# A macaron layer on one core: later sums for the first pair of quarters in the first FFN, and plain products for the second pair in its fourth chunk

## The chip, the core and the metric

The kernel runs on one core of one Trainium2 chip. The time is the device time of that core in microseconds (us), from the first to the last instruction with what lies around it. The kernel before takes 2368.13 us, the median of three runs (2365.34 to 2368.92).

The engines named below: TensorE (PE in the rows; PEld is its weight load), VectorE (DVE), ScalarE (ACT), GpSimd (POOL), and SyncE (SP), whose queue issues all DMAs of this kernel.

## The reference, cut to what matters

One encoder layer is applied to 1024 prompt frames and 32 sample frames, side by side as 1056 columns of 1024 channels. Its first step, where the change lies, is a half-step SwiGLU FFN:

```python
def _swiglu_half_step(x, g_pre, g_post, w_in, w_out):
    h = _rmsnorm(x, g_pre)
    gate, up = jnp.split(h @ w_in, 2, axis=-1)
    return x + 0.5 * _rmsnorm((jax.nn.silu(gate) * up) @ w_out, g_post)
```

D_FF is 2816, so `w_in` gives 22 chunks of 128 gate rows and 128 up rows. All inputs are float32. After this FFN come a mixing part (convolution and RG-LRU branches), a second FFN of the same form and a last norm.

## The kernel before

**Precision.** Each float32 operand is split into a high part and a low part (`split`, L84: ScalarE copies the high part, then VectorE subtracts it from the operand). A product is three matmuls (`mm3`, L204 to L206): high by high, high by low, low by high.

**Columns.** The 1056 columns are four quarters of 264 (q = 0 to 3); quarters 0 and 1 are the first pair, 2 and 3 the second.

**Two ways to form a chunk.** *Plain products* (`gemm`): for each quarter the gate row and the up row take 8 k-steps each, so one pair of quarters costs 2 x 2 x 8 x 3 = 96 matmuls. They read the chunk's two weight blocks, each split over 1024 columns into `wh_i`, `wl_i`. *Seven products* (`swiglu`): a pair of quarters is treated as a 2 x 2 block product with seven instead of eight block products, 7 x 4 x 3 = 84 matmuls. They need seven weight operands (`w_ops`, `w1` to `w7`) and seven column operands `xh1`..`xh7`, `xl1`..`xl7` of the pair. Parts 1, 2 and 3 are split from the normed quarters; 4 to 7 come from sums of them (`x_sums`: four sums into `t` or `f`, each followed by a split). `swiglu` runs the products in the order 1, 5, 6, 2, 7, 3, 4 on four PSUM banks; a copy on ScalarE and an add on VectorE stand between them.

**The first FFN's start.** The first three chunks (`NP[0]` = 3) take plain products for all four quarters, quarter by quarter, while the operands of the other 19 are made. Quarters 0 and 1 go in with only the gain applied; their norm factor is put in afterwards on the products (`held`, `rows`), and their column parts are built later (`build`, with `f_a0`, `f_a1`). Quarters 2 and 3 are normed first: squares on ScalarE (`sq_a`), their sum on VectorE (`ss_a`), a matmul with ones (`pst`, L230), `r_a` on VectorE, a power on GpSimd (`q_a`, L234), a transpose on TensorE (`pst`, L240), then eight multiplications (`f_a`, L270) and the splits. Quarter 3's first half is split into `xhp`, `xlp` (needed by the plain products) and its second into `xh3`, `xl3`.

**What sets the order.** The program's order is a priority: a scheduler keeps it on each engine except where `tc.high_priority`, `tc.issue_after` or free buffers move an instruction. So what the loop over q emits first on VectorE is first there. `x_sums` of the first pair (with the builds before it) is emitted after quarter 1's products, and `first(3, h)`, quarter 3's norm, is emitted at the start of quarter 2's turn:

```python
            late = first(q + 1, h) if q + 1 < NQ else None
            ...
            c = {1: 0, 3: 1}.get(q) if n == 1 else {2: 0, 3: 1}.get(q)
            if c is not None:
                while builds:
                    builds.pop(0)()
                x_sums(x[c], f[2 * c], f[2 * c + 1], f"{n}_{c}")
```

**Buffers.** Raw weight blocks have 3 buffers (`w_i`, `w_g`, `w_u`), split weights a ring of 12 (`NRING`), PSUM banks 6. A DMA on the SP queue waits there until its buffer is free, and everything behind it waits too. `WAHEAD` and `WLATE` say how far ahead of its place a chunk's `w_ops` is put.

Of the kernel before, what the change touches and what calls it, by code (L numbers as in the profile page):

```python
# [10 lines left out]
AF = mybir.ActivationFunctionType  # L11
OP = mybir.AluOpType
# [8 lines left out]
N = T // NQ  # L21
# [15 lines left out]
AHEAD, WAHEAD, WLATE, HAHEAD, OAHEAD, EAHEAD = 350, 120, 100, 100, 150, 200  # L37
# [17 lines left out]
def macaron_kernel(ctx: ExitStack, tc: tile.TileContext, a: dict, o: dict):  # L55
    nc = tc.nc
# [26 lines left out]
    def TMP(name):  # L83
        return tp.tile([P, N], F32, tag="t", name=name)  # L84
# [4 lines left out]
    def tt(out, x, y, op):  # L89
        return nc.vector.tensor_tensor(out, x, y, op=op)  # L90
# [125 lines left out]
    def gemm(blk, h, q, name):  # L216
        b = BANK(name)[:, :N]
        while q not in h:
            later.pop(0)[1]()
        for k in range(KC):  # L220
            hi, lo = h[q][k // HC]
            mm(b, blk, k, hi[:, k % HC, :], lo[:, k % HC, :], k == 0, k == KC - 1)
        return b
# [132 lines left out]
    def x_sums(r, fe, fo, name):  # L356
        t = QUAD(F32, f"t_{name}")

        def op(k, v):
            r[k] = (QUAD(F32R, f"xh{k}_{name}"), QUAD(F32R, f"xl{k}_{name}"))  # L360
            split(*r[k], v)

        tt(t, fo[0], fe[0], OP.subtract)
        op("5", t)
        tt(t, fo[1], t, OP.subtract)
        op("6", t)
        tt(fo[0], fo[1], fo[0], OP.subtract)
        op("7", fo[0])
        tt(t, fe[1], t, OP.subtract)
        op("4", t)  # L370

    def w_ops(g, u, name, ahead):
        r = {}
        with tc.high_priority(offset=ahead):
            wg, wu = raw_block(g, f"g{name}"), raw_block(u, f"u{name}")
            H = D // 2
            a11, a12, a21, a22 = wg[:, :H], wg[:, H:], wu[:, :H], wu[:, H:]

            def op(k, v):
                r[k] = ring.tile([P, 2, H], F32R, tag="r", name=f"w{k}_{name}")  # L380
                split(r[k][:, 0, :], r[k][:, 1, :], v)

            def mid(n):
                return mp.tile([P, H], F32, tag="m", name=f"{n}_{name}", padded_shape=[P, 2 * N])

            op("1", a11)
            op("2", a12)
            op("4", a22)
            s = mid("s")
            tt(s, a21, a22, OP.add)  # L390
            op("5", s)
            tt(s, s, a11, OP.subtract)
            op("6", s)
            s3 = mid("s3")
            tt(s3, a11, a21, OP.subtract)
            tt(s, a12, s, OP.subtract)
            op("7", s3)
            op("3", s)
        return r
# [64 lines left out]
    def ffn(x, f, h, first, mid, w_in, w_out, early, between, finish, tail, n):  # L464
        hd = dp.tile([NF, P, T], F32, name=f"hd{n}")

        def hidden(i, w, cs):
            cols = [(x[c], MID(f"prod{n}_{i}_{c}")) for c in cs]
            last = swiglu(w, cols, f"{n}_{i}_{cs[0]}")
            for c, (_, prod) in zip(cs, cols):  # L470
                nc.sync.dma_start(hd[i, :, 2 * N * c:2 * N * (c + 1)], prod)
            return last

        blks = []

        def in_block(i, j):
            blks.append(block(w_in[2 * i + j], f"i{n}_{i}_{j}", AHEAD if n == 2 else 0, 0 if n == 2 else 2000 if i or j else 4000))

        if n == 1:
            late = first(0, h, lambda: in_block(0, 0))  # L480
        else:
            late = first(0, h)
        q0 = list(newest_part) if n == 1 else []
        np = NP[n - 1]
        for i in range(np):
            for j in range(2):
                if 2 * i + j == len(blks):
                    with behind_parts(q0):
                        in_block(i, j)
        held, rows = {}, {}  # L490
        for q in range(NQ):
            if late:
                held[q] = []
                late(held, rows)
            late = first(q + 1, h) if q + 1 < NQ else None
            if q not in h:
                drain()
            for i in range(np):
                pg = gemm(blks[2 * i], h, q, f"pg{n}_{i}_{q}")
                pu = gemm(blks[2 * i + 1], h, q, f"pu{n}_{i}_{q}")  # L500

                def gate(i=i, q=q, pg=pg, pu=pu, rows=rows):
                    t = TMP(f"si{n}_{i}_{q}")
                    if q in held:
                        u = TMP(f"su{n}_{i}_{q}")
                        tt(t, rows[q], pg, OP.mult)
                        tt(u, rows[q], pu, OP.mult)
                        pg, pu = t, u
                    nc.scalar.activation(t, pg, AF.Silu)
                    tt(t, t, pu, OP.mult)  # L510
                    nc.sync.dma_start(hd[i, :, q * N:(q + 1) * N], t)

                if q in held and q not in rows:
                    held[q].append(gate)
                else:
                    gate()
            c = {1: 0, 3: 1}.get(q) if n == 1 else {2: 0, 3: 1}.get(q)
            if c is not None:
                while builds:
                    builds.pop(0)()  # L520
                x_sums(x[c], f[2 * c], f[2 * c + 1], f"{n}_{c}")
        for i in range(np, NF):
            with behind_parts(q0 if i == np else []):
                w = w_ops(w_in[2 * i], w_in[2 * i + 1], f"{n}_{i}", WAHEAD if i < np + 2 else WLATE)
            for cs in ((0,), (1,)) if i == np else ((0, 1),):
                end = hidden(i, w, cs)
            if i == 4:
                with tc.issue_after(end):
                    mid()

        sq = {}
        for c in range(2):
            hid = []
            for g in range(NF // 2):
                with tc.high_priority(offset=HAHEAD):
                    w = PAIR(F32, f"hf{n}_{c}_{g}")
                    nc.sync.dma_start(w, hd[2 * g:2 * g + 2, :, 2 * N * c:2 * N * (c + 1)].rearrange("k p n -> p k n"))
                    hi, lo = PAIR(F32R, f"hh{n}_{c}_{g}"), PAIR(F32R, f"hl{n}_{c}_{g}")
                    split(hi, lo, w)
                hid.append((hi, lo))  # L540
            y = {q: [QUAD(F32, f"y{n}_{q}_{h}") for h in range(2)] for q in (2 * c, 2 * c + 1)}
            for t in (t for q in y for t in y[q]):
                nc.gpsimd.memset(t[:, 0, 0:1], 0.0)
            if c == 1:
                for q in y0:
                    after(q * STAG, lambda q=q, y0=y0: early(q, y0[q], sq[q]))
            y0 = y

            def out(tiles, blks, which, c=c, hid=hid, y=y):

                b = {t: BANK(f"po{n}_{t[0]}_{t[1]}")[:, :N] for t in tiles}
                for k in range(NF):
                    hi, lo = hid[k // 2]
                    for m, q in tiles:
                        i = m * NF + k
                        if i // KC not in blks:
                            blks[i // KC] = block(w_out[i // KC], f"o{n}_{which}_{i // KC}", OAHEAD)
                        s = slice((q % 2) * N, (q % 2 + 1) * N)
                        mm(b[m, q], blks[i // KC], i % KC, hi[:, k % 2, s], lo[:, k % 2, s], k == 0, k == NF - 1)
                for m, q in tiles:  # L560
                    evacuate(y[q], m, b[m, q], half[:, n - 1, m:m + 1], sq, q, f"{n}_{q}_{m}")

            qs = (2 * c, 2 * c + 1)
            late = tail if c == 1 else 0
            both = {}
            out([(m, q) for m in range(OG) for q in qs], both, c)
            for m in range(OG, KC - late):
                for q in qs:
                    out([(m, q)], both, c)
                if c == 1 and m == HC - 1:  # L570
                    between()
            for q in qs:
                own = {}
                for m in range(KC - late, KC):
                    out([(m, q)], own, f"{c}_{q}")
                if c == 1 and q == 2:
                    finish(q, y[q], sq[q])
        return lambda: finish(3, y[3], sq[3])
# [62 lines left out]
    rows = {}  # L641
# [39 lines left out]
    w_in = a["w_in"]  # L681
# [81 lines left out]
    for i in range(KC):  # L763
# [3 lines left out]
        if first:  # L767
            u = ROW(F32, f"u{i}")
# [27 lines left out]
        else:  # L796
            u = ROW(F32, f"u{i}")
# [156 lines left out]
    for c in range(2):  # L954
        blks = {}
# [4 lines left out]
        for q in (2 * c, 2 * c + 1):  # L960
            blks = {}
# [75 lines left out]
```

## Time and profile before

| | us |
|---|---|
| median of three runs | 2368.13 |
| the profiled execution | 2366.67 |
| its span, first to last instruction | 2364.9 |
| TensorE busy in the span | 2323.3 (98%) |
| VectorE, ScalarE, GpSimd busy | 1466.2, 988.5, 41.6 |

The profiled execution lies 1.46 us under the median and 1.8 us over its own span. Its mean granted TensorE clock is 0.993 of full speed. A matmul's duration in the rows (0.28 us) overlaps its neighbours', so its cost is the distance from start to start. In the rows of a timeline the columns are start, duration, engine, line, operation, output and inputs, shapes, count, and in brackets the idle time before it with what ended it.

### The profile page before, as it was taken

How to read it: one execution, taken by the hardware profiler on the slowest of the kernel's cores; microseconds unless marked ns; L12 is line 12 of the kernel's file. 1: busy time of each engine (PE TensorE's matmuls, PEld its weight loads, DVE VectorE, ACT ScalarE, POOL GpSimd, SP SyncE). 2: the span in 40 equal slices, each digit the busy share in tenths (PEclk: the TensorE clock that was granted, in tenths of full speed). 3: DMA queues.
4: the chain of work that ended last, by engine and by line, in shares of the span. 5: the costliest groups of instructions: out<-in, count | busy, mean ns of one | idle time of the engine just before them, and what ended most of it. 6: DMA issues, size and time to landing. Idle time of an engine off the chain costs nothing.

```text
span 2364.9 us, 44868 instructions
## 1 busy us (share of the span) xinstructions
PE 2323.3 (98%) x19136; PEld 2318.4 (98%) x19136; DVE 1466.2 (62%) x2289; ACT 988.5 (42%) x1709; POOL 41.6 (2%) x63
## 2 busy tenths in 40 slices
PE   8799999999999999999999999999999999999996
PEld 8799999999999999999999999999999999999996
DVE  6764444542656887887778966458744444552646
ACT  4443333442444554355543434244433333442432
POOL 0000000000000000000000000001000000000000
PEclk9899999999999999999999999999999999999998
DMA  4122222353656222222122554444222222353554
GB/s 173 50 83 82 76 79 82 106 195 116 202 184 192 74 82 78 70 90 83 65 72 84 184 192 157 146 135 154 77 74 78 82 79 76 120 188 108 169 173 130
DMA packets 126088, 274.12 MB, mean 116 GB/s; under 512 B 16704, under 2 KB 58432, under 8 KB 125888
## 3 DMA queue, kind: packets, MB, share of 16 engines
q1 hardware_dynamic: 125888, 271.26, 34.3%
q8 instruction: 149, 2.44, 0.4%
q14 instruction: 51, 0.42, 0.1%
HBM read 212.55 MB, written 58.67 MB: 115 GB/s over the span
## 4 chain that ended last, share of the span: by engine, by line
PE 95%; DVE 2%; issue 1%; DMA 1%; ACT 0%; POOL 0%; SPq 0%; POOLq 0%; DVEq 0%
PE p L204 11%; PE p L206 11%; PE p L205 11%; PE po L205 7%; PE po L204 7%; PE po L206 7%; PE pm L204 3%; PE pm L206 3%; PE pm L205 3%; PE pcv L204 1%; PE pco L204 1%; PE pcg L204 1%; PE pro L204 1%; PE prx L204 1%; PE prg L204 1%; PE pcg L206 1%
## 5 line engine op out<-in xcount | busy, mean ns | idle before, releaser
L206 PE MATMUL p<-xh,w 128*128 128x264 f32 x2184 | 617.4, 283 | 0.0
L205 PE MATMUL p<-xl,w 128*128 128x264 f32 x2184 | 617.3, 283 | 0.0
L204 PE MATMUL p<-xh,w 128*128 128x264 f32 x2184 | 614.5, 284 | 0.0
L205 PEld LDWEIGHTS p<-xl,w 128*128 128x128 f32 x2184 | 410.8, 188 | 0.0
L206 PEld LDWEIGHTS p<-xh,w 128*128 128x128 f32 x2184 | 410.2, 188 | 0.0
L204 PEld LDWEIGHTS p<-xh,w 128*128 128x128 f32 x2184 | 407.8, 188 | 0.4 <-ACT p L93 0.2
L205 PE MATMUL po<-hl,wh_o 128*128 128x264 f32 x1408 | 398.0, 285 | 0.2
L206 PE MATMUL po<-hh,wl_o 128*128 128x264 f32 x1408 | 396.6, 284 | 0.0
L204 PE MATMUL po<-hh,wh_o 128*128 128x264 f32 x1408 | 391.7, 286 | 0.0
L205 PEld LDWEIGHTS po<-hl,wh_o 128*128 128x128 f32 x1408 | 264.8, 188 | 0.9 <-DVE hl L90 0.9
L206 PEld LDWEIGHTS po<-hh,wl_o 128*128 128x128 f32 x1408 | 264.4, 188 | 0.0
L204 PEld LDWEIGHTS po<-hh,wh_o 128*128 128x128 f32 x1408 | 260.8, 188 | 0.3 <-ACT hh L93 0.2
L90 DVE TENSOR_TENSOR wl_o<-w_o,wh_o 128x1024 fp32r<-128x1024 f32 x109 | 133.0, 1223 | 117.2 <-ACT wh_o L93 116.9
L90 DVE TENSOR_TENSOR p<-p,s 128x264 f32<-128x264 f32 x78 | 34.2, 441 | 273.0 <-ACT p L93 273.0
L709 DVE SCALAR_TENSOR_TENSOR pq<-u,vec,pq 128x542 f32<-128x542 f32 (+14 forms) x232 | 170.7, 767 | 0.0
L93 ACT ACTIVATE wh_o<-w_o 128x1024 fp32r<-128x1024 f32 x109 | 115.3, 1063 | 121.5 <-PE po L205 111.6
L90 DVE TENSOR_TENSOR w<-s,w 128x512 fp32r<-128x512 f32 x156 | 104.4, 690 | 76.3 <-ACT w L93 76.1
L93 ACT ACTIVATE p<-p 128x264 f32<-128x264 f32 x156 | 58.3, 374 | 198.1 <-PE p L206 197.0
L93 ACT ACTIVATE w<-s 128x512 fp32r<-128x512 f32 x156 | 94.0, 626 | 81.7 <-DVE s L90 79.1
L709 DVE SCALAR_TENSOR_TENSOR rs<-rs,wsum 128x542 f32<-128x542 f32 (+6 forms) x112 | 86.0, 768 | 0.0
L90 DVE TENSOR_TENSOR s<-s,s 128x264 f32<-128x264 f32 x56 | 24.0, 429 | 99.1 <-ACT s L315 98.9
L90 DVE TENSOR_TENSOR hl<-hf,hh 128x1056 fp32r<-128x1056 f32 x44 | 55.2, 1254 | 44.5 <-ACT hh L93 44.4
(465 smaller groups left out, 5680.8 us busy)
## 6 DMA issues: line engine op xcount, KB each, us to landing
w_o<-in_w_ffn_out SPq DMA_DIRECT2D x109, 512.0 KB, 3.7
hf<-hd SPq DMA_DIRECT2D x44, 528.0 KB, 4.9
hd<-prod SPq DMA_DIRECT2D x78, 264.0 KB, 2.0
w_g<-in_w_ffn_in SPq DMA_DIRECT2D x39, 512.0 KB, 3.5
w_u<-in_w_ffn_in SPq DMA_DIRECT2D x39, 512.0 KB, 3.4
w_wo<-in_w_out SPq DMA_DIRECT2D x18, 512.0 KB, 3.6
sgd<-sg SPq DMA_DIRECT2D x32, 264.0 KB, 2.5
gs<-sgd SPq DMA_DIRECT2D x16, 528.0 KB, 6.7
```

The costliest lines, as they stand in the source:

```text
L90: return nc.vector.tensor_tensor(out, x, y, op=op)
L93: return nc.scalar.activation(out, x, AF.Copy)
L204: nc.tensor.matmul(out, wh, xh, start=first, stop=False, skip_group_check=True)
L205: nc.tensor.matmul(out, wh, xl, start=False, stop=False, skip_group_check=True)
L206: newest_mm[:] = [nc.tensor.matmul(out, wl, xh, start=False, stop=last, skip_group_check=True).ins]
L709: nc.vector.scalar_tensor_tensor(acc[c][:, d:], src[c][:, :HW - d], wt[c](d), acc[c][:, d:], op0=OP.mult, op1=OP.add)
```

## The change

In the first FFN the first pair's builds and sums are emitted after quarter 2's products instead of after quarter 1's. The second FFN already had that place. The body that forms a plain chunk becomes a function `plain(i, q)`, the same lines as before. After the loop over the quarters, two more blocks of weights (the fourth chunk's, `i` = 3) are loaded and split, and that chunk takes plain products for quarters 2 and 3; its seven products are then run for the first pair alone. The chunk that runs its two pairs one after the other instead of interleaved is now the fifth.

```diff
             for i in range(np):
...
-            c = {1: 0, 3: 1}.get(q) if n == 1 else {2: 0, 3: 1}.get(q)
+                plain(i, q)
+            c = {2: 0, 3: 1}.get(q)
             if c is not None:
                 while builds:
                     builds.pop(0)()
                 x_sums(x[c], f[2 * c], f[2 * c + 1], f"{n}_{c}")
+        both = np
+        if n == 1:
+
+            both = np + 1
+            for j in range(2):
+                in_block(np, j)
+            for q in (2, 3):
+                plain(np, q)
         for i in range(np, NF):
             with behind_parts(q0 if i == np else []):
-                w = w_ops(w_in[2 * i], w_in[2 * i + 1], f"{n}_{i}", WAHEAD if i < np + 2 else WLATE)
-            for cs in ((0,), (1,)) if i == np else ((0, 1),):
+                w = w_ops(w_in[2 * i], w_in[2 * i + 1], f"{n}_{i}", WAHEAD if i < both + 2 else WLATE)
+            for cs in ((0,),) if i < both else ((0,), (1,)) if i == both else ((0, 1),):
                 end = hidden(i, w, cs)
```

**VectorE, from the end of quarter 1 to the sum of squares of quarter 3.** In the names `f_a1`, `sq_a3` the digit is the quarter; `xl5_1_0` is part 5 of the first pair in the first FFN. Before:

```order
L270 SCALAR_TENSOR_TENSOR f_a1_1_660<-x0_1_1_90,vec_87,rb_a1_506 128x264 x4
L90 TENSOR_TENSOR xl3_1_1_666<-f_a1_1_660,xh3_1_1_665 128x4x264
L90 TENSOR_TENSOR t_1_0_669<-f_a1_0_655,f_a0_0_637 128x4x264
L90 TENSOR_TENSOR sq_a3_0_690<-sq_a3_0_690,sq_a3_2_692 128x528
L90 TENSOR_TENSOR f_a1_0_655<-f_a1_1_660,f_a1_0_655 128x4x264
L90 TENSOR_TENSOR xl5_1_0_672<-t_1_0_669,xh5_1_0_671 128x4x264
L90 TENSOR_TENSOR sq_a3_0_690<-sq_a3_0_690,sq_a3_4_695 128x528
L90 TENSOR_TENSOR t_1_0_669<-f_a1_1_660,t_1_0_669 128x4x264
```

The changed kernel has there, on VectorE:

```order
L90 TENSOR_TENSOR su1_2_1_631<-rb_a1_506,pu1_2_1_605 128x264
L90 TENSOR_TENSOR sq_a3_0_637<-sq_a3_0_637,sq_a3_2_639 128x528
L90 TENSOR_TENSOR si1_2_1_630<-si1_2_1_630,su1_2_1_631 128x264
L90 TENSOR_TENSOR sq_a3_0_637<-sq_a3_0_637,sq_a3_4_642 128x528
L90 TENSOR_TENSOR sq_a3_0_637<-sq_a3_0_637,sq_a3_6_645 128x528
L90 TENSOR_TENSOR ss_a3_648<-sq_a3_0_637 128x264
L232 TENSOR_SCALAR r_a3_692<-pst_a3_688 88x3
L90 TENSOR_TENSOR si1_0_2_708<-si1_0_2_708,pu1_0_2_675 128x264
L270 SCALAR_TENSOR_TENSOR f_a3_0_722<-x0_3_0_177,vec_87,pst_a3_688 128x264 x4
L90 TENSOR_TENSOR xlp_1_3_728<-f_a3_0_722,xhp_1_3_727 128x4x264
```

Quarter 3's squares and its `f_a3` now stand directly behind quarter 1's last gate; the builds of quarters 0 and 1 and all sums of the first pair stand behind them.

With them quarter 3's ones-matmuls (`pst`, L230) and transposes (L240) on TensorE move from behind quarter 2's last product into its first products, some 100 matmuls forward.

**VectorE, in the fourth chunk's seven products for the first pair, in the changed kernel.** `w7_1_3` and `w3_1_3` are weight operands of the fourth chunk (chunk index 3), `w1_1_4` of the fifth; `p6`, `p7` are PSUM banks; `xl6_1_1` to `xl4_1_1` are parts of the second pair.

```order
L90 TENSOR_TENSOR w7_1_3_1222<-s3_1_3_1219,w7_1_3_1222 128x512
L90 TENSOR_TENSOR xl6_1_1_1064<-t_1_1_1056,xh6_1_1_1063 128x4x264
L90 TENSOR_TENSOR si1_3_2_1139<-si1_3_2_1139,pu1_3_2_1114 128x264
L90 TENSOR_TENSOR p6_1_3_0_0_1242<-p6_1_3_0_0_1242,s5_1_3_0_0_1257 128x264
L90 TENSOR_TENSOR xl7_1_1_1069<-f_a3_0_722,xh7_1_1_1068 128x4x264
L90 TENSOR_TENSOR t_1_1_1056<-f_a2_1_539,t_1_1_1056 128x4x264
L90 TENSOR_TENSOR prod1_3_0_1228<-p7_1_3_0_0_1271,s5_1_3_0_0_1257 128x264
L90 TENSOR_TENSOR w3_1_3_1225<-s_1_3_1210,w3_1_3_1225 128x512
L90 TENSOR_TENSOR w1_1_4_1333<-w_g1_4_1329,w1_1_4_1333 128x512
```

Splits of the second pair stand between the steps that this chunk's products wait for; before, the second pair's last split stands in front of the chunk's first step.

**SP, the queue of DMAs.** The two new weight loads are put among the loads of quarters 2 and 3:

```order
 L174 DMA w_i_2_1_167<-in_w_ffn_in 128x1024
+L174 DMA w_i_3_0_1077<-in_w_ffn_in 128x1024
 L113 DMA x_2_0_173<-in_x 128x4x264
+L174 DMA w_i_3_1_1083<-in_w_ffn_in 128x1024
 L113 DMA x_2_1_174<-in_x 128x4x264
```

Three of the four loads of x (quarter 2's second half and quarter 3) now stand behind two weight loads, the first half of quarter 2 behind one. The order of TensorE from the sixth chunk's first product on is the same row by row.

## Rows read from the trace of the kernel before

**Rows 1.** The page, part 1: busy time, share of the span, instructions.

```profile
PE 2323.3 (98%) x19136; PEld 2318.4 (98%) x19136; DVE 1466.2 (62%) x2289; ACT 988.5 (42%) x1709; POOL 41.6 (2%) x63
```

**Rows 2.** Waits of TensorE up to 300 us: waiter, releaser, us in total, times, longest.

```profile
PE pst_a L230 <- DVE ss_a L90: 8.0, 1, 8.0
PE pg L204 <- ACT xhp L93: 2.9, 1, 2.9
PE pst_a L240 <- POOL q_a L234: 1.2, 1, 1.2
```

**Rows 3.** Timeline of TensorE, 48 to 141 us, where stages begin or end.

```profile
48.21 0.29 PE L204 MATMUL pg<-xh,wh_i 128*128 128x264 f32 x1
...
65.53 0.28 PE L206 MATMUL pu<-xh,wl_i 128*128 128x264 f32 x1
...
73.80 1.01 PE L230 MATMUL pst_a<-ones,ss_a 128*88 128x1 f32 x6 [7.99 <-DVE ss_a L90]
...
79.65 0.59 PE L204 MATMUL pg<-xhp,wh_i 128*128 128x264 f32 x1 [2.90 <-ACT xhp L93]
...
99.61 0.29 PE L204 MATMUL p<-xh,w 128*128 128x264 f32 x1
...
140.33 0.29 PE L204 MATMUL p<-xh,w 128*128 128x264 f32 x1
```

**Rows 4.** Timeline of VectorE, 62 to 74 us.

```profile
62.51 1.25 DVE L90 TENSOR_TENSOR t<-f_a,f_a 128x1056 f32<-128x1056 f32 x1
63.68 0.70 DVE L90 TENSOR_TENSOR sq_a<-sq_a,sq_a 128x528 f32<-128x528 f32 x1
...
73.22 0.42 DVE L90 TENSOR_TENSOR ss_a<-sq_a 128x264 f32<-128x264 f32 x1
```

**Rows 5.** Windows: stretch, length, busy time (instructions) by engine, granted clock, DMA.

```profile
65.80:79.65 13.85, 1.72 (x11) 1.39 (x10) 12.54 (x20) 5.06 (x7) 0.85 (x1) 0.69 0.03 10
79.65:84.85 5.20, 5.20 (x23) 5.06 (x24) 3.99 (x6) 1.08 (x1) 0.00 (x0) 0.51 0.17 55
```

**Rows 6.** Timeline of TensorE, 23 to 27 us: a norm's matmuls among products.

```profile
23.34 0.56 PE L230 MATMUL pst_a<-ones,ss_a 128*88 128x1 f32 x6
...
23.96 0.28 PE L205 MATMUL pg<-gl,wh_i 128*128 128x264 f32 x1
...
26.02 0.39 PE L240 MATMUL pst_a<-ident,q_a 88*128 88x88 f32 x3
...
26.41 0.28 PE L205 MATMUL pu<-gl,wh_i 128*128 128x264 f32 x1
```

**Rows 7.** Timeline of VectorE: builds at 56.86 us, gate and weight splits near 89 us.

```profile
56.86 3.31 DVE L270 SCALAR_TENSOR_TENSOR f_a<-x,vec,rb_a 128x264 f32<-128x264 f32 x8
...
89.11 0.42 DVE L90 TENSOR_TENSOR si<-si,pu 128x264 f32<-128x264 f32 x1
89.44 0.68 DVE L90 TENSOR_TENSOR w<-w_g,w 128x512 fp32r<-128x512 f32 x1
90.05 0.68 DVE L90 TENSOR_TENSOR w<-w_u,w 128x512 fp32r<-128x512 f32 x1
```

**Rows 8.** Timeline of SP, 18 to 22 us: loads that waited for a raw buffer.

```profile
18.79 0.84 SPq L174 DMA_DIRECT2D w_g<-in_w_ffn_in  x1
21.36 0.34 SPq L174 DMA_DIRECT2D w_u<-in_w_ffn_in  x1
```

**Rows 9.** Instructions on the tile x, its last line: loads, issue to landing.

```profile
DMA to landing us min/median/max: 3.0/6.4/8.8
```

**Rows 10.** Timeline of ScalarE, 30 to 32 us: squares of quarter 2.

```profile
30.39 1.17 ACT L260 ACTIVATE sq_a<-x 128x528 f32<-128x528 f32 x2
```

**Rows 11.** Timeline of TensorE at 1639 us: a short wait late in the run.

```profile
1639.34 0.44 PE L240 MATMUL pst_e<-ident,q_e 88*128 88x88 f32 x3 [1.42 <-POOL q_e L234]
```

**Rows 12.** Window behind that wait, columns as in rows 5.

```profile
1639.40:1645.00 5.60, 5.60 (x49) 5.60 (x50) 4.43 (x11) 1.48 (x2) 0.77 (x1) 1.00 0.33 114
```

**Rows 13.** Waits of VectorE, 40 to 145 us.

```profile
DVE xl L90 <- ACT xh L93: 5.1, 5, 1.2
```

More of the change, by code (lines that the diff above doesn't have):

```diff
@@ L490, in ffn, with plain, gate @@
         held, rows = {}, {}
+        def plain(i, q):
+            pg = gemm(blks[2 * i], h, q, f"pg{n}_{i}_{q}")
+            pu = gemm(blks[2 * i + 1], h, q, f"pu{n}_{i}_{q}")
+            def gate(pg=pg, pu=pu):
+                t = TMP(f"si{n}_{i}_{q}")
+                if q in held:
+                    u = TMP(f"su{n}_{i}_{q}")
+                    tt(t, rows[q], pg, OP.mult)
+                    tt(u, rows[q], pu, OP.mult)
+                    pg, pu = t, u
+                nc.scalar.activation(t, pg, AF.Silu)
+                tt(t, t, pu, OP.mult)
+                nc.sync.dma_start(hd[i, :, q * N:(q + 1) * N], t)
+            if q in held and q not in rows:
+                held[q].append(gate)
+            else:
+                gate()
         for q in range(NQ):
@@ L498, in ffn @@
             for i in range(np):
[L499 to L516, printed above, removed]
-            c = {1: 0, 3: 1}.get(q) if n == 1 else {2: 0, 3: 1}.get(q)
+                plain(i, q)
+            c = {2: 0, 3: 1}.get(q)
             if c is not None:
```

## The prediction, made before the changed kernel was run

> **What bounds the kernel now.** The page's first part comes first: TensorE is busy 98% of the span [rows 1], so a change pays only by removing TensorE instructions or TensorE's idle time. Next its waits in the first 300 us: apart from the first weight's arrival there are three, and they form one hole, 8.0 us for the sum of squares `ss_a`, 1.2 us for GpSimd's power, 2.9 us for the split `xhp` [rows 2]. They are the steps of quarter 3's norm. The timeline places it: quarter 2's products begin at 48.21, its last matmul starts at 65.53, quarter 3's first product at 79.65, the fourth chunk's at 99.61, the sixth chunk's at 140.33 [rows 3]. From 99.61 on 336 matmuls (two chunks of 2 x 84) take 40.72 us: 0.121 us each, start to start, and that is the price of a matmul below (its 0.28 us overlaps the neighbours').
>
> Why is `ss_a` late? VectorE's timeline shows its three adds between the first pair's sums (a sum at 62.51, an add at 63.68) and `ss_a` itself at 73.22, long after quarter 3's x landed [rows 4]. VectorE is busy 12.5 of the hole's 13.85 us [rows 5]. The hole has a tail: in it and behind it the granted clock falls to 0.69 and 0.51, the lower level of 1.2 GHz, for another 5.2 us [rows 5].
>
> **The hole goes.** In the changed order quarter 3's squares stand directly behind quarter 1's last gate. VectorE gets there when quarter 1's last product is done, which is when quarter 2's first starts (48.21); three adds of 0.7 and three short steps take it to about 51.5. TensorE reaches the ones-matmuls after 36 products, at 52.6, the transposes at 55.0. Four builds (1.7), a copy on ScalarE (VectorE waits 5.1 us for five such now [rows 6], so 1.0 to 1.15 each), a split, four builds, a split: quarter 3's operands are there by 63.6. Quarter 2's products end at 48.21 + 144 x 0.121 + 0.8 = 66.4. So TensorE goes on without a wait, 2.8 us of slack. The 0.8 is what the norm's nine small matmuls cost among products: 23.34 to 23.96 less one matmul is 0.50, 26.02 to 26.41 less one is 0.27 [rows 7].
>
> - Hole: 79.65 - 65.65 = 14.0, less 0.8: 13.2 us saved.
> - Half clock: quarter 3's 144 matmuls take 99.61 - 79.65 = 19.96 us; at full clock 17.44: 2.5 us saved.
> - Plain products instead of seven for one pair: 96 - 84 = 12 matmuls more, 12 x 0.121 = 1.45 us lost.
>
> Together 14.3 us, before new waits.
>
> **New waits.** The first pair's builds and sums are not gone; they now follow quarter 3's norm and must be ready when the fourth chunk's seven products start. TensorE gets there at 66.4 + 144 x 0.121 + 96 x 0.121 = 95.5: the plain products for the second pair buy 11.6 us, since they need only parts 1, 2, `p` and 3 and the two new weight splits. VectorE's bill from 63.6 to the last weight operand (`w3`) of that chunk: 16 builds of 0.41 (eight take 3.31), 18 sums and splits of 1056 columns of 1.17 (62.51 to 63.68, [rows 4]), two new weight splits of 1024 at no more than that, 11 weight steps of 512 at 0.61 (89.44 to 90.05), 7 gate steps of 264 at 0.33 (89.11 to 89.44) [rows 8]: 6.6 + 21.1 + 2.3 + 6.7 + 2.3 = 39.0. VectorE also idles about 1.2 us for quarter 2's last product and 0.7 us for the first new block's copy, which needs the buffer that the first chunk frees. It has `w3` ready at 104.5. TensorE wants it in the sixth of seven products, at 95.5 + 5 x 1.45 = 102.8. So VectorE is late by 1.7 us, the least that the waits can be. Within these chunks each product also waits for short steps behind longer ones: the add into bank 7 stands behind a split and a sum of the second pair (2 x 1.17), and the banks of the two plain gates come free only with their gates. Going through the new order of the engines row by row, with these prices and the banks free, I get 3.6 us of waits in the fourth and fifth chunk; with banks taken strictly in turn 5.1. I take 4.5. (The same walk over the order before restarts quarter 3 at 78.6; the trace has 79.65.) The upper end is 8: three more waits of a split for its copy, 1.15 each, as the trace has them where no other work lies between. After the sixth chunk's first product the order on TensorE is the same row by row and moves as a block.
>
> **The inputs.** The two new blocks are loaded among the x loads, and each waits for a raw buffer: the buffers come free at 18.79 and 21.36 [rows 9]. Quarter 2's second half is then issued near 21.8 and lands within the longest 8.8 us [rows 10], by 30.6; its squares before ran from about 31 (the pair that starts at 30.39 is one of each half) [rows 11]. I cost it at nothing, covered by the gates and squares of quarters 0 and 1; if the cover fails, TensorE waits at quarter 2's norm, up to 3 us. Quarter 3's x has 15 us to spare. The two loads and the two ScalarE copies fall into time where DMA and ScalarE stand mostly idle (0.03 of DMA, 5.06 of 13.85 us [rows 5]).
>
> **Sum.** 14.3 - 4.5 = 9.8 us. The profiled execution's 2366.67 gives 2356.9; it lies 1.46 under the median, so against 2368.13 the forecast is 2358.3, with 1.7 to 8 us of waits 2355.5 to 2361.8.
>
> **A rule against the change.** The new waits are short pauses between groups of matmuls on rotating banks. The trace has one such: 1.42 us at 1639.34 [rows 12], and the granted clock behind it is 1.00 [rows 13]; so the sum has no clock term. In the Trainium skill, "TensorE: Matmul & The Clock Gate", section "A second HAM failure mode: psum-queue depth-cycling", a kernel that cycles through PSUM banks leaves TensorE idle for moments so often that its clock swings between both levels. By the rule the waits would bring half clock back; by the row not, but that is one pause and here there may be six. No run so far shows six together.
>
> **Rivals.**
> - *No new waits (0.12).* VectorE overlaps better than I walked it; for it, the walk's waits are each under 2 us; against it, VectorE's bill alone leaves 1.7. 2354 to 2355.5.
> - *The clock falls again (0.12).* Two falls, each worth the 2.5 us found above, on top of 4.5: 2363.3. For it, six pauses within 20 us; against it, the row at 1639. This is what the skill's rule would give.
> - *Quarter 2's x comes late (0.06).* 3 us at the ones-matmuls of quarter 2: 2361.
> - *VectorE and ScalarE never catch up (0.04): slower.* In the fourth and fifth chunk all ten splits since quarter 3's norm wait 1.15 for their copies, as five do now (5.1 us [rows 6]): 11.5 us more, with two clock falls 5 more. 4.5 + 11.5 + 5 = 21 against 14.3: 2374.8. It decides from about 14 us of waits. Against it: between copy and split the new order has other work nearly everywhere.
>
> That the change does not do what it says has no chance that I count: the rows of the order show both moves.
>
> **Chances.** Forecast 0.66, rivals as above. A measurement of this kernel can tell 0.2% (4.7 us) from no change, so "faster" means under 2363.4. The forecast, the first and the third rival lie there (0.84), and a third of the second (0.04): 0.88. The rest of the second, 0.08, is no change; 0.04 slower. The range: 2353.5 (no waits, the runs' own scatter) to 2363.5 (clock falls).
>
> **What would show it.** Right: no TensorE wait between 48 and 95 us; quarter 3's first product near 66; granted clock 1.00 throughout; the sixth chunk's first product near 130.5 instead of 140.33; waits of TensorE between 100 and 120 for VectorE's `w`, `prod` and ScalarE's copies `p`, 2 to 8 us in all. Wrong: a wait for `ss_a` or `xhp` that remains, a wait at quarter 2's norm, half clock after 100, or a sixth chunk that starts after 136.

## The result, and the profile after

One correction first: from 6 on, the group numbers cited in the prediction are out of step with the groups shown ahead of it. Its "rows 6" (VectorE's waits of 1.0 to 1.15 us for copies) is [rows 13], and its "rows 7" to "rows 13" are [rows 6] to [rows 12], each one lower. Below, groups are named as they stand.

The changed kernel takes 2355.59 us (median of 4 runs, 2354.88 to 2356.62) against 2368.11 for the kernel before beside it: a ratio of 0.995, 95% interval 0.9932 to 0.9967. The forecast was 2358.3 in a range from 2353.5 to 2363.5, and faster: right, with 12.5 us of gain where 9.8 were forecast. The time alone does not tell the forecast (2355.5 with the least waits) from the rival without new waits (up to 2355.5); the trace does. The profiled execution took 2356.62 us, 10.05 less than that of before; its span is 10.9 us shorter.

The page's part 1 of the changed kernel, which answers to [rows 1]:

```profile
PE 2323.5 (99%) x19148; PEld 2317.8 (98%) x19148; DVE 1467.3 (62%) x2289; ACT 988.6 (42%) x1708; POOL 39.9 (2%) x63
```

The 12 matmuls more are there, and TensorE's busy time is the same within 0.2 us: what went is idle time. TensorE's waits up to 160 us (waiter, releaser, us in total, times, longest), against [rows 2]:

```profile
PE pg L204 <- ACT wh_i L93: 8.2, 1, 8.2
PE p L204 <- DVE prod L90: 0.8, 1, 0.8
PE p L204 <- ACT p L93: 0.7, 2, 0.5
PE pg L206 <- DVE wl_i L90: 0.5, 1, 0.5
PE p L206 <- DVE w L90: 0.2, 1, 0.2
```

The first and the fourth line are the start of the program, as before. The three for `ss_a`, `q_a` and `xhp` are gone, and three small ones are new. They stand between 104 and 116 us in TensorE's timeline (start, duration, what; in brackets the idle time and its releaser), which answers to [rows 3]:

```profile
48.85 0.28 PE L204 MATMUL pg<-xh,wh_i 128*128 128x264 f32 x1
...
67.05 0.28 PE L204 MATMUL pg<-xhp,wh_i 128*128 128x264 f32 x1
...
84.49 0.28 PE L204 MATMUL pg<-xh,wh_i 128*128 128x264 f32 x1
...
96.12 0.28 PE L204 MATMUL p<-xh,w 128*128 128x264 f32 x1
...
104.87 0.39 PE L204 MATMUL p<-xh,w 128*128 128x264 f32 x1 [0.84 <-DVE prod L90]
...
109.48 0.39 PE L204 MATMUL p<-xh,w 128*128 128x264 f32 x1 [0.47 <-ACT p L93]
...
113.08 0.39 PE L206 MATMUL p<-xh,w 128*128 128x264 f32 x1 [0.17 <-DVE w L90]
...
115.27 0.39 PE L204 MATMUL p<-xh,w 128*128 128x264 f32 x1 [0.23 <-ACT p L93]
...
129.49 0.28 PE L204 MATMUL p<-xh,w 128*128 128x264 f32 x1
```

Read the stages off it: quarter 2 begins at 48.85, quarter 3 at 67.05 (79.65 before), the fourth chunk's plain products at 84.49, its seven products at 96.12, the sixth chunk at 129.49. That is 10.84 us earlier than 140.33, the span's whole difference. Quarter 3's 144 matmuls take 84.49 - 67.05 = 17.44 us; before they took 19.96.

VectorE shows why quarter 3 needs no wait. Its timeline, which answers to [rows 4]:

```profile
49.40 0.70 DVE L90 TENSOR_TENSOR sq_a<-sq_a,sq_a 128x528 f32<-128x528 f32 x1
50.02 0.42 DVE L90 TENSOR_TENSOR si<-si,su 128x264 f32<-128x264 f32 x1
50.36 1.51 DVE L90 TENSOR_TENSOR sq_a<-sq_a,sq_a 128x528 f32<-128x528 f32 x2
51.91 0.43 DVE L90 TENSOR_TENSOR ss_a<-sq_a 128x264 f32<-128x264 f32 x1
...
63.17 1.26 DVE L90 TENSOR_TENSOR xl<-f_a,xh 128x1056 fp32r<-128x1056 f32 x1 [0.81 <-ACT xh L93]
```

`ss_a` starts at 51.91 instead of 73.22, and the last split of quarter 3 ends at 64.4, 2.6 us before TensorE wants the quarter. The windows of the stages behind it (columns as in [rows 5]):

```profile
66.00:84.00 18.00, 18.00 (x150) 18.00 (x150) 16.13 (x26) 9.21 (x13) 0.00 (x0) 1.00 0.16 53
84.00:95.50 11.50, 11.50 (x97) 11.50 (x96) 11.49 (x14) 5.17 (x8) 0.00 (x0) 1.00 0.32 103
95.50:110.00 14.50, 13.19 (x107) 12.77 (x106) 14.43 (x21) 8.80 (x16) 0.00 (x0) 1.00 0.25 80
```

The granted clock stays at 1.00 where [rows 5] had 0.69 and 0.51. VectorE (the third busy time) has no free time from 84 to 110 us. Of TensorE's four waits two end with VectorE's steps (`prod`, `w`) and two with ScalarE's copies of a bank (`p`). The longest, 0.84 us, ends with the add that reads bank 7, which on VectorE stands behind a split and a sum of the second pair:

```profile
102.06 1.25 DVE L90 TENSOR_TENSOR xl<-f_a,xh 128x1056 fp32r<-128x1056 f32 x1
103.22 1.25 DVE L90 TENSOR_TENSOR t<-f_a,t 128x1056 f32<-128x1056 f32 x1
104.39 0.42 DVE L90 TENSOR_TENSOR prod<-p,s 128x264 f32<-128x264 f32 x1
```

### The profile page after: what moved, and what is told of

Read it like the earlier page. It is cut to its first block, busy times and chain, and to the rows that moved or that the text cites. A ratio compares the mean times of both kernels' runs of the same rounds, so it can differ in the third digit from the quotient of the medians.

```text
span 2354.0 us, 44900 instructions
## 1 busy us (share of the span) xinstructions
PE 2323.5 (99%) x19148; PEld 2317.8 (98%) x19148; DVE 1467.3 (62%) x2289; ACT 988.6 (42%) x1708; POOL 39.9 (2%) x63
## 4 chain that ended last, share of the span: by engine, by line
PE 93%; DVE 3%; DMA 1%; issue 1%; ACT 1%; POOL 0%; SPq 0%; POOLq 0%; DVEq 0%
PE p L204 11%; PE p L206 11%; PE p L205 11%; PE po L205 7%; PE po L204 7%; PE po L206 7%; PE pm L204 3%; PE pm L206 3%; PE pm L205 3%; PE pcv L204 1%; PE pco L204 1%; PE pcg L204 1%; PE pro L204 1%; PE prx L204 1%; PE prg L204 1%; PE prg L206 1%
## 5 line engine op out<-in xcount | busy, mean ns | idle before, releaser
L206 PE MATMUL p<-xh,w 128*128 128x264 f32 x2156 | 609.4, 284 | 0.2 <-DVE w L90 0.2
L205 PE MATMUL p<-xl,w 128*128 128x264 f32 x2156 | 609.4, 283 | 0.0
L204 PE MATMUL p<-xh,w 128*128 128x264 f32 x2156 | 607.1, 284 | 1.5 <-DVE prod L90 0.8
L205 PEld LDWEIGHTS p<-xl,w 128*128 128x128 f32 x2156 | 405.6, 188 | 0.0
L206 PEld LDWEIGHTS p<-xh,w 128*128 128x128 f32 x2156 | 404.9, 188 | 0.4 <-DVE w L90 0.4
L204 PEld LDWEIGHTS p<-xh,w 128*128 128x128 f32 x2156 | 402.6, 188 | 2.6 <-ACT p L93 1.3
L90 DVE TENSOR_TENSOR wl_o<-w_o,wh_o 128x1024 fp32r<-128x1024 f32 x109 | 132.9, 1222 | 116.5 <-ACT wh_o L93 116.2
L90 DVE TENSOR_TENSOR p<-p,s 128x264 f32<-128x264 f32 x77 | 33.7, 440 | 267.3 <-ACT p L93 267.3
L93 ACT ACTIVATE wh_o<-w_o 128x1024 fp32r<-128x1024 f32 x109 | 115.3, 1063 | 121.4 <-PE po L205 114.1
L90 DVE TENSOR_TENSOR w<-s,w 128x512 fp32r<-128x512 f32 x156 | 104.5, 689 | 72.6 <-ACT w L93 72.1
L93 ACT ACTIVATE p<-p 128x264 f32<-128x264 f32 x154 | 57.5, 374 | 194.4 <-PE p L206 194.4
L93 ACT ACTIVATE w<-s 128x512 fp32r<-128x512 f32 x156 | 94.1, 626 | 80.8 <-DVE s L90 78.1
L90 DVE TENSOR_TENSOR s<-s,s 128x264 f32<-128x264 f32 x56 | 23.9, 429 | 98.7 <-ACT s L315 98.5
L90 DVE TENSOR_TENSOR hl<-hf,hh 128x1056 fp32r<-128x1056 f32 x44 | 55.2, 1254 | 46.4 <-ACT hh L93 46.2
```

Source lines behind the costliest of these rows:

```text
L93: return nc.scalar.activation(out, x, AF.Copy)
L204: nc.tensor.matmul(out, wh, xh, start=first, stop=False, skip_group_check=True)
L205: nc.tensor.matmul(out, wh, xl, start=False, stop=False, skip_group_check=True)
L206: newest_mm[:] = [nc.tensor.matmul(out, wl, xh, start=False, stop=last, skip_group_check=True).ins]
```

## The experiments

Two landmarks serve in all of them: quarter 3's first product, and the sixth chunk's first, behind which all orders do the same work. Between them lie 480 matmuls, or 492 with the plain chunk; at 0.1212 us each (40.72 / 336) that is 58.17 or 59.63 us. What the trace has above that is waits and half clock, called the excess. For the changed kernel: 129.49 - 67.05 = 62.44, an excess of 2.8 us. (The idle times in the brackets add up to 1.7. They count from the modelled end of the matmul before, 0.28 us behind its start, where the next would start after 0.12: 0.16 more for each wait. The matmul behind a wait then takes 0.22 us to the next, 0.10 more than usual. Together 1.7 + 0.6 + 0.4.)

| kernel | median us (before beside it) | quarter 3 at | to the sixth chunk | excess | from there to the last matmul |
|---|---|---|---|---|---|
| before | 2368.11 | 79.65 | 60.68 | 2.5 | 2217.7 |
| changed | 2355.59 (2368.11) | 67.05 | 62.44 | 2.8 | 2217.9 |
| changed again | 2357.02 (2368.87) | 67.24 | 62.44 | 2.8 | 2218.6 |
| sums alone | 2356.85 (2369.17) | 67.33 | 61.29 | 3.1 | 2219.6 |
| sums alone again | 2358.13 (2368.87) | 67.38 | 61.28 | 3.1 | 2221.5 |
| plain products alone | 2368.45 (2369.17) | 78.75 | 62.44 | 2.8 | 2220.5 |
| late second sums | 2354.66 (2369.17) | 66.24 | 60.97 | 1.3 | 2217.5 |
| late again | 2355.39 (2368.87) | 66.92 | 61.10 | 1.5 | 2219.2 |
| more for VectorE | 2358.15 (2369.17) | 66.21 | 64.52 | 4.9 | 2220.0 |
| late sums, no plain | 2363.65 (2368.87) | 67.13 | 65.81 | 7.6 | 2222.1 |
| sums alone, a memset | 2355.9 (2367.81) | 66.11 | 61.46 | 3.3 | 2220.0 |
| changed, a memset | 2355.38 (2367.81) | 65.98 | 62.46 | 2.8 | 2217.5 |

**The move of the sums alone.** The kernel before with one line changed:

```diff
-            c = {1: 0, 3: 1}.get(q) if n == 1 else {2: 0, 3: 1}.get(q)
+            c = {2: 0, 3: 1}.get(q)
```

> The kernel before with one edit: the first pair's builds and sums follow quarter 2's products; the fourth chunk keeps seven products for both pairs. Nothing of the computation is left out. Theory A (the place of the sums is all of the gain, the plain products are hardly needed): going through the order row by row with the prices of the trace before, quarter 3's first product comes at 66.2 to 66.6 us with no wait before it, the fourth chunk's first at 83.6 to 84.1, and TensorE waits 2.5 to 4.5 us in short pieces in the fourth and fifth chunk, because the second pair's products that need only parts already made stand between. The sixth chunk starts at 84 + 40.7 + 3.5 = 128.2 us (after: 129.45, before: 140.33); one execution 2353.5 to 2355.5 us, equal to or up to 2 us better than the changed kernel. Theory B (the plain products are needed: they buy 11.6 us for VectorE): VectorE has w3 ready at 63.6 + 39.0 - 2.3 + 1.9 = 102.2 us, TensorE wants it at 84.0 + 5 x 1.45 = 91.2 us; 11 us of waits between 84 and 105 us, with half clock behind them 2 us more; sixth chunk at 136 to 138 us, 2362 to 2364 us, less than half of the gain.

Measured: 2356.85 us, ratio 0.9945 (0.9933 to 0.9958): 12.3 us under before, as the changed kernel, and 1.35 us over the expected band (before beside it is 1.1 us slower here than in the first comparison). TensorE's timeline:

```profile
67.33 0.29 PE L204 MATMUL pg<-xhp,wh_i 128*128 128x264 f32 x1
...
91.24 0.39 PE L204 MATMUL p<-xh,w 128*128 128x264 f32 x1 [0.50 <-ACT p L93]
...
102.10 0.39 PE L205 MATMUL p<-xl,w 128*128 128x264 f32 x1 [0.91 <-DVE xl L90]
...
128.62 0.29 PE L204 MATMUL p<-xh,w 128*128 128x264 f32 x1
```

No wait of 11 us: theory A holds, and the place of the sums is the gain. The bill of 39.0 us that made the plain products look necessary counted seven sums and splits of the second pair (7 x 1.17 = 8.2 us) which the first pair's products don't need. In this kernel's order on VectorE those stand behind the first pair's last weight operand.

**The plain products alone.** The changed kernel with the sums back at their old place:

```diff
-            c = {2: 0, 3: 1}.get(q)
+            c = {1: 0, 3: 1}.get(q) if n == 1 else {2: 0, 3: 1}.get(q)
```

> The changed kernel with the first pair's builds and sums back behind quarter 1's products, so that the plain products for the second pair stand alone. Nothing is left out. Theory A (the hole is made by the sums ahead of quarter 3's norm): the wait for ss_a stays (about 8 us), quarter 3's first product comes at 79.5 to 81 us, the granted clock falls behind it, and no wait stands in the fourth chunk; 12 matmuls more cost 12 x 0.121 = 1.45 us: sixth chunk at 141.5 to 143 us, 2367.5 to 2370.5 us, not faster than before. Rival (the plain products by themselves bring part of the gain, since they unload VectorE where it is late): sixth chunk before 139 us, 2360 to 2365 us.

Measured: 2368.45 us, ratio 0.9997 (0.9988 to 1.0005): no gain. TensorE's timeline and then the two windows of the hole:

```profile
69.91 0.60 PE L230 MATMUL pst_a<-ones,ss_a 128*88 128x1 f32 x6 [3.92 <-DVE ss_a L90]
73.17 0.70 PE L240 MATMUL pst_a<-ident,q_a 88*128 88x88 f32 x3 [2.65 <-POOL q_a L234]
78.75 0.59 PE L204 MATMUL pg<-xhp,wh_i 128*128 128x264 f32 x1 [4.89 <-ACT xhp L93]
```

```profile
65.90:78.70 12.80, 1.40 (x10) 0.98 (x9) 11.39 (x17) 5.06 (x7) 1.81 (x1) 0.70 0.09 32
78.70:84.50 5.80, 5.75 (x25) 5.62 (x26) 4.56 (x7) 1.08 (x1) 0.00 (x0) 0.50 0.01 3
```

The hole is there, and the half clock behind it, so theory A holds. Its parts moved: 3.9 us for `ss_a` where about 8 were expected, but more for the power and the split behind it, since VectorE does splits, a sum and gates of other work between those steps. Quarter 3 starts at 78.75, a little before the expected 79.5. A hole is better forecast as a whole than by its parts.

**The second pair's sums later.** The changed kernel, the second pair's sums emitted behind the fourth chunk's seven products for the first pair:

```diff
-            if c is not None:
+            if c is not None and (n == 2 or c == 0):
...
             for cs in ((0,),) if i < both else ((0,), (1,)) if i == both else ((0, 1),):
                 end = hidden(i, w, cs)
+            if n == 1 and i == np:
+                x_sums(x[1], f[2], f[3], f"{n}_1")
```

> The changed kernel with the second pair's sums and splits emitted behind the fourth chunk's seven products for the first pair. Nothing is left out. Theory A (the 2.8 us of waits that are left between 104 and 116 us come from the second pair's splits, which stand in front of the steps that the fourth chunk waits for): the waits there fall under 1 us, the sixth chunk starts near 127.5 us (after: 129.45), 2354.5 us or less in the profiled execution. Rival B (VectorE has the same work before the fifth chunk's second pair, so other waits of the same size stand there): waits of 2.5 to 4 us between 100 and 128 us, now for the second pair's parts; sixth chunk at 129 to 131 us, 2356 to 2358 us.

Measured: 2354.66 us, ratio 0.9937 (0.9923 to 0.9951). TensorE's timeline has two waits, neither of them at a product where the changed kernel has one of its four:

```profile
66.24 0.28 PE L204 MATMUL pg<-xhp,wh_i 128*128 128x264 f32 x1
...
98.76 0.39 PE L204 MATMUL p<-xh,w 128*128 128x264 f32 x1 [0.39 <-ACT p L93]
...
115.71 0.39 PE L204 MATMUL p<-xh,w 128*128 128x264 f32 x1 [0.31 <-DVE prod L90]
...
127.21 0.29 PE L204 MATMUL p<-xh,w 128*128 128x264 f32 x1
```

The excess falls from 2.8 to 1.3 us. The wait for `prod`, the only one of the four that the rows above show behind a split and a sum of the second pair, is gone, as theory A has it; its "under 1 us" was missed. Rival B is right that other waits come and wrong in their size; the one at 115.71 is again for that add, in the fifth chunk. The saving is not the splits' alone: in this program's order TensorE runs nearly every product of the two chunks whole, where the changed kernel's runs neighbours into each other, and ScalarE's two waits are gone with that order. How the 1.5 us divide is not shown.

**More work for VectorE.** The changed kernel with four copies ahead of the first pair's builds:

```diff
             if c is not None:
+                if c == 0 and n == 1:
+                    for k in range(4):
+                        nc.vector.tensor_copy(f[3][1], f[3][1])
```

> The changed kernel with four more copies of 1056 columns of an operand onto itself on VectorE, among the first pair's builds; the values stay as they are. At the price of a sum (1.17 us) that is 4.7 us more for VectorE, all of it behind quarter 3's split and ahead of the fourth chunk's seven products. In the changed kernel's trace VectorE is busy 16.13 of 18.0 us from 66 to 84, 11.49 of 11.50 from 84 to 95.5 and 14.43 of 14.50 from 95.5 to 110. Theory A (VectorE's bill sets the waits): beyond the 1.9 us of idle time it comes through one to one: TensorE waits 2.8 to 4.7 us more between 84 and 116 us, the sixth chunk starts at 132.2 to 134.2 us, 2359.4 to 2361.3 us. Rival B (the waits come from the order of short steps behind long ones, VectorE's total has slack): under 1 us more, sixth chunk before 130.5 us, 2356 to 2357.6 us.

Measured: 2358.15 us; sixth chunk at 130.73, which lies between both expectations. The price of a copy was wrong. VectorE's copies (median duration in ns in the middle), and the window of the waits:

```profile
L524 DVE COPY f_a<-f_a x4: 701/702/702, 63.9 to 66.9; 128x1056 f32<-128x1056 f32 x4
```

```profile
100.00:117.00 17.00, 14.68 (x103) 12.78 (x102) 16.46 (x25) 11.13 (x21) 0.00 (x0) 1.00 0.46 131
```

Four copies are 2.8 us by their durations (2.5 from start to start, 0.62 each), not 4.7. Quarter 3 starts 0.84 us earlier in this trace, so VectorE's idle time is read from the landmark: from 5 us before quarter 3's first product to the fourth chunk's first it is busy 20.47 instead of 19.76 us. So 0.7 us went into idle time, and 1.8 to 2.1 us should come through: the excess rose by 4.9 - 2.8 = 2.1 (64.52 against 62.44 us between the landmarks). With the copy's own price theory A holds, and "under 1 us" is refuted: what VectorE gets more to do from 64 us on, TensorE waits for. The two waits for ScalarE's copies stay at 0.47 and 0.23 us; they are not set by VectorE's load.

**One chip, four orders.** The changed kernel and the two variants above once more, unchanged, and a fourth: the sums alone with the second pair's sums emitted between the fourth chunk's two runs.

> The changed kernel once more, on the same chip as the next three. Two questions. First, the 0.64 us by which its quarter 2 started later than before: in the five traces of the changed orders the 31st matmul starts between 14.1 and 15.3 us, and from there to quarter 3's first product it is 52.0 to 52.1 us in all of them. Theory A (scatter of the first 15 us, not the change): the 31st matmul starts anywhere from 14.1 to 15.4 us, the 52.0 stay. Theory B (the two weight loads among the x loads delay the start): it starts at 14.9 us or later again. Second, the waits between 84 us and the sixth chunk: 2.8 us again if the order sets them, within 0.3 us. 2355 to 2358 us.

> The kernel with the second pair's sums behind the fourth chunk's seven products, once more, beside the changed kernel on one chip. Theory A (the waits for the second pair's splits were real and are gone): waits 1.2 to 1.6 us against 2.8, and from quarter 3's first product to the sixth chunk's first 61.0 us against 62.4; the median 1 to 2.5 us under the changed kernel's. Rival (what the first run gained was scatter of the start): the medians agree within 0.5 us.

> The move of the sums alone, once more, beside the changed kernel on one chip. From quarter 3's first product to the sixth chunk's it took 61.29 us against 62.44 in the changed kernel: 12 matmuls fewer (1.45 us), waits 3.05 against 2.78 us. Theory A (the plain products cost what their matmuls cost and save almost no wait): 61.0 to 61.6 us again, the median 0.5 to 1.5 us under the changed kernel's. Rival (something later in the program gives it back, as the first run's end suggests, where the rest from the sixth chunk on took 2219.6 against 2217.9 us): the rest is 1.5 us longer again, and the medians agree within 0.5 us.

```diff
             for cs in ((0,), (1,)) if i == np else ((0, 1),):
+                if n == 1 and cs == (1,):
+                    x_sums(x[1], f[2], f[3], f"{n}_1")
                 end = hidden(i, w, cs)
```

> Before with both cheap edits: the first pair's sums behind quarter 2's products, no plain products, and the second pair's sums emitted between the fourth chunk's seven products for the first pair and those for the second. Nothing is left out. Theory A (without plain products the second pair's sums are needed at once, whatever place they are emitted from): waits of 2.5 to 4 us as in the move alone, 61 to 62 us from quarter 3's first product to the sixth chunk's, 2354.5 to 2357 us. Rival B (late emission takes the waits away here too): 1.2 to 1.8 us of waits, 59.5 to 60 us, and the fastest of all, 2352.5 to 2354 us.

*Changed again:* the excess is 2.8 us once more, and the four waits stand in the same places. The start is scatter: the 31st matmul begins at 15.22 us here, 15.08 in the first trace, 14.49 before, but also 14.14 with the sums late, which has the same two weight loads among the x loads, and 15.34 with the sums alone, which has not. What scatters is how many of the first matmuls stand 0.22 us apart instead of 0.12: 15 in the trace of before, 19 and 24 in the two of the changed kernel, 10 to 24 in all twelve. Theory A.

*Late again:* excess 1.5 us, 1.34 us less between the landmarks; the median is 1.6 us under the changed kernel's. The difference between the landmarks is shown in two pairs of traces; the medians agree with it, but their intervals against before (0.9928 to 0.9953, and 0.9935 to 0.996) overlap. It has the lowest median of its group both times, so it is the one to keep, though the medians alone do not prove it.

*Sums alone again:* 61.28 us between the landmarks as expected, but the median is 1.1 us over the changed kernel's, not under it. The rival was right in kind: the rest of the program takes 2221.5 us against 2218.6, more than the 1.5 us it named. Row against row from the sixth chunk on, three jumps recur in both traces of this order: 0.8 us near 726 us, 1.5 to 1.7 near 1628 us and 0.5 to 0.65 near 2216 us. The first two are waits of TensorE for GpSimd's power, and the last section returns to them; the third is a wait for a split on VectorE.

*Late sums without plain products:* both theories missed. Between the landmarks theory A expected 61 to 62 us, rival B 59.5 to 60; measured are 65.81, and 2363.65 us, ratio 0.998 (0.997 to 0.999). Theory A is right that the second pair's sums are needed at once and wrong that their place does not matter. TensorE's waits and the windows around the longest:

```profile
97.27 0.39 PE L204 MATMUL p<-xh,w 128*128 128x264 f32 x1 [0.46 <-ACT p L93]
...
99.69 0.39 PE L205 MATMUL p<-xl,w 128*128 128x264 f32 x1 [0.42 <-DVE xl L90]
...
103.18 0.59 PE L204 MATMUL p<-xh,w 128*128 128x264 f32 x1 [1.88 <-ACT xh L93]
...
104.56 0.59 PE L205 MATMUL p<-xl,w 128*128 128x264 f32 x1 [0.80 <-DVE xl L90]
```

```profile
101.00:104.50 3.50, 0.89 (x4) 0.37 (x2) 3.47 (x5) 2.85 (x4) 0.00 (x0) 0.72 0.48 150
104.50:109.50 5.00, 4.93 (x22) 4.94 (x23) 4.02 (x7) 1.59 (x5) 0.00 (x0) 0.51 0.00 2
109.50:114.00 4.50, 4.50 (x39) 4.50 (x38) 4.24 (x8) 3.38 (x7) 0.00 (x0) 1.00 0.35 117
```

Here the second pair's products follow at once, and late sums make them wait; TensorE is busy 0.89 of 3.50 us, and behind that the clock is at its lower level of 1.2 GHz for 5 us (22 matmuls at 0.22 us). So this is what the plain products buy: room to place the second pair's sums late. Alone, the late emission costs 4.5 us between the landmarks (65.81 against 61.28), about 2.5 of them the half clock; with the plain products it saves 1.4.

**One memset more on GpSimd.** To find what sets the length of GpSimd's power, the sums alone and the changed kernel each got this at the start:

```diff
     make_identity(nc, ident)
+    pad = cp.tile([P, 1], F32, name="pad")
+    nc.gpsimd.memset(pad, 0.0)
```

> The move of the sums alone, with one more instruction on GpSimd, a memset of one column of an unused tile at the program's start. The question is GpSimd's power of 88x3 for the norm: the same instruction lasts 0.85 to 2.48 us, and its eighteenth in order of time before the end (q_e of the third quarter) lasted 2.48 us in the four traces without the plain chunk, where TensorE then waits 1.4 us for it, and 1.36 to 1.37 us in the six with it. Theory A (the length goes with the place in GpSimd's instruction stream): with all places moved by one, the long ones fall on other instructions; q_e takes another length than 2.48 us, and where it falls to 1.4 us or less, TensorE's wait near 1628 us is gone and the rest from the sixth chunk on is 1.5 us shorter than 2219.6 to 2221.5 us. Theory B (the length goes with what the other engines do beside it): 2.45 to 2.5 us again, with the wait.

> The changed kernel with the same additional memset on GpSimd at the start. Theory A (place in the stream): the lengths of the powers change against the changed kernel's two traces, which agree with each other to 0.02 us; some that lasted 0.85 us last 1.8 us and the other way round, and the time moves by up to 2 us either way. Theory B (what stands beside it): the same lengths as before, q_e 1.36 us, and 2355 to 2358 us.

Measured: 2355.9 us and 2355.38 us, with 2367.81 for before beside them. The power in question on GpSimd, first the sums alone with the memset, then the changed kernel with it:

```profile
1625.91 2.48 POOL L236 TENSOR_TENSOR q_e<-r_e,mhalf 88x3 f32<-88x3 f32 x1 [6.49 <-DVE r_e L234]
```

```profile
1625.71 1.36 POOL L236 TENSOR_TENSOR q_e<-r_e,mhalf 88x3 f32<-88x3 f32 x1 [6.26 <-DVE r_e L234]
```

The lengths do not move with the place in GpSimd's stream: theory A is refuted. Theory B is what remains of the two, and the last section reads from the traces which neighbour it is.

## Why the prediction was right, and where its sizes were off

- **The hole, 13.2 us: right.** Quarter 2's first product to quarter 3's takes 67.05 - 48.85 = 18.20 us, and 66.4 - 48.21 = 18.2 was forecast. `ss_a` was forecast to end by about 51.5 and starts at 51.91; the 2.8 us of slack are 2.6. The two experiments with one part each show that the place of the sums does this and the plain products do not.
- **Half clock, 2.5 us: right,** 19.96 - 17.44.
- **Twelve matmuls, 1.45 us: right.** The plain products take 96.12 - 84.49 = 11.63 us (11.6 forecast).
- **New waits: the step that was mis-sized,** 2.8 us against 4.5 (bounds 1.7 to 8). The kind was right: the waits are for `prod`, `w` and ScalarE's copies `p`, as forecast, and the longest is the add from bank 7 behind a split and a sum of the second pair (103.22 - 102.06 and 104.39 - 103.22, the 2 x 1.17 of the prediction). The 4.5 lay between 3.6 with banks free and 5.1 with banks taken strictly in turn; the trace lies under the first. That banks cost nothing does not follow, since three of the four waits end with a step that reads a bank. `w3` was forecast for 104.5, and VectorE finishes it at 104.73 + 0.68 = 105.4; but TensorE's order runs the last two products into each other, so that at 104.87 it waits 0.84 us for `prod` and not at all for `w3`. The "least" of 1.7 was reckoned against a strict order of products that the kernel does not have.
- **The plain products "buy 11.6 us": wrong as a need.** VectorE's bill took in the second pair's work; without the plain products the excess is 3.1 instead of 2.8 us. Between the landmarks they cost 62.44 - 61.28 = 1.2 us.
- **The inputs: right.** There is no wait at quarter 2's norm, and the start that came 0.64 us later than before is scatter of the first 15 us.
- **Rivals.** *No new waits* is out, by 2.8 us. *VectorE never catches up* needed ten waits for copies as in [rows 13]; the changed kernel's line for it (`DVE xl L90 <- ACT xh L93`) reads 1.3 us in 2 waits. *The clock falls again* did not happen: 1.00 over the four waits, and 1.00 too with six waits (0.20 to 0.65 us) from 102 to 117 us when VectorE had more to do. What the Trainium skill ("TensorE: Matmul & The Clock Gate", "A second HAM failure mode: psum-queue depth-cycling") reports of a kernel, that short idle moments between groups swing the clock, did not happen in these two traces. But the rival was no phantom: with late sums and no plain products the half clock came back. It came inside the wait of 1.88 us that ends at 103.18: the granted clock reads 1.00 from 101.0 to 102.5 us and 0.50 from 102.6 on. In the kernel before, the wait in which the clock fell is 7.99 us [rows 3]; the four pauses of the changed kernel are 0.84 us at most.

The sum for the profiled execution: 9.8 forecast, + 1.7 for the waits, - 0.64 for the scatter of the start, makes 10.9, the span's difference. What lies around the span was 2.6 us instead of 1.8, which leaves 10.05. The median's 12.5 is larger because this execution lies 1.0 above its median and that of before 1.4 below: about 2.5 us of the 12.5 are scatter of that kind. In the second group of runs the gain was 2368.87 - 2357.02 = 11.85.

## What to carry to other kernels

A wait is removed by what stands in front of it in an engine's order, and the price is paid where the displaced work is due: bill only the work that the next consumer needs, row by row, and not all that was displaced. When an engine has no free time in the stretch that follows, what it gets more to do shows up on the engine that waits for it: here 2.1 us of 2.8. The pauses of up to 0.84 us left the granted clock at 1.00; the three standstills behind which it fell (before, plain products alone, late sums without plain products) cost 2.5 to 2.8 us more than their length.

## What had not been expected of the hardware

GpSimd's power of 88x3 is one instruction of one shape, and it lasts from 0.84 to 2.48 us. Its length at a given place repeats from execution to execution, mostly to 0.02 us, and differs between orders of the other engines. The one between 1624 and 1641 us took 2.48 us in all five traces without the plain chunk and 1.35 to 1.37 in all seven with it. GpSimd's timeline of before and, second, of the changed kernel, each with the row of VectorE's timeline whose end it follows:

```profile
1637.88 0.70 DVE L90 TENSOR_TENSOR sq_e<-sq_e,sq_e 128x528 f32<-128x528 f32 x1
1636.81 2.48 POOL L234 TENSOR_TENSOR q_e<-r_e,mhalf 88x3 f32<-88x3 f32 x1 [6.57 <-DVE r_e L232]
```

```profile
1626.67 0.71 DVE L90 TENSOR_TENSOR sq_e<-sq_e,sq_e 128x528 f32<-128x528 f32 x1
1626.72 1.36 POOL L234 TENSOR_TENSOR q_e<-r_e,mhalf 88x3 f32<-88x3 f32 x1 [6.26 <-DVE r_e L232]
```

The power ends at 1639.29 and 1628.08, that row of VectorE at 1638.58 and 1627.38: 0.71 and 0.70 us earlier. The same holds throughout. The twelve traces have 384 such powers. The 209 short ones take 0.84 to 0.85 us, and in 201 of them no instruction of VectorE is running when the power begins (in the other eight one that ends within 0.3 us). In the 175 longer ones an instruction of VectorE is running, and the power ends 0.70 to 0.73 us behind the end of an instruction of VectorE: of that same one in 170, of a later one in the five of 2.48 us. So the neighbour is VectorE. This is read from the times; no run moved VectorE's instruction alone, and why five powers outlast three instructions where the others outlast one is not shown.

This is the power behind the wait of [rows 11], and the changed kernel's row for the same transposes has none:

```profile
1628.14 0.44 PE L240 MATMUL pst_e<-ident,q_e 88*128 88x88 f32 x3
```

So the statement that everything behind the sixth chunk's first product moves as a block was not quite right (nor is the order there the same in every row: nine matmuls of the sixth chunk stand elsewhere in it). The wait is gone, 1.5 us row against row, and as much was lost in small pieces elsewhere: the rest took 2217.9 us against 2217.7. The two waits for a long power, 2.3 to 2.5 us together, are more than the 1.2 us by which the move alone is ahead up to the sixth chunk, and so it was no faster in the end. The place in GpSimd's stream does not set the length; where the power falls among VectorE's instructions does, as far as these traces tell.
